# Making the remainder of each weight tile with an adding DMA instead of a subtraction

## The chip, the cores and the metric

The kernel runs on one core of a Trainium2 chip. The metric is the device time of one execution in microseconds; the time of a kernel is the median of several runs. Five engines work side by side, each through its own instructions in order: PE (matmul, with PEld for its weight loads), DVE (vector), ACT (scalar), POOL (GpSimd) and SP (which here only issues DMAs). POOL and ACT can issue DMAs too.

## The reference

The reference is the trunk of a two-layer transformer over 512 latent tokens and 256 context tokens, width 1024, in float32. Cut to its frame:

```
for layer in range(2):
    h_x = modulate(rmsnorm(x), ...);  h_c = modulate(rmsnorm(ctx), ...)
    o_x, o_c = attention(h_x @ w_in, h_c @ w_in) @ w_out
    x = x + gate * o_x
    h_x = modulate(rmsnorm(x), ...)
    x = x + gate * ((silu(h_x @ w1) * (h_x @ w3)) @ w2)
    if layer == 0:                      # the same two updates for ctx
        ...
return rmsnorm(x, final_g)
```

Layer 0 has two kinds of attention side by side (differential heads and neighbourhood heads), layer 1 a windowed grouped-query attention with sinks. The modulation vectors come from one matrix product per layer (`ada_w`).

## The kernel before

**Precision.** Each large matrix product in float32 is made of three matmuls in a rounded 32-bit format (`F32R` in the code, fp32r in the profile). A weight tile is split into a rounded part `wh` and a remainder `wl` = tile − `wh`; an activation is split likewise. `mm3` then adds up, for each block of 128 rows, `wh`·high (L157), `wh`·low (L158) and `wl`·high (L159). In the first attention unit the same three products stand as L475 to L477 (key, query) and L483 to L485 (value); for values L341 to L343.

**Weight tiles.** The class `Stream` brings all weights in one fixed order. A tile is 128 x 1024 floats, 512 KB. `request` issues its load on SP (L126) into a buffer `raw`; `make` splits it; `next` hands it out and keeps two tiles ahead of the matmuls (`ahead=2`). `wpool` has three buffers for each of `raw`, `wh` and `wl`; the tiles of `w2` have their own four buffers of `wh` and `wl`, but the same three of `raw`. A buffer of `wh` or `wl` comes free when PE has used the tile three places earlier; one of `raw` when the tile in it has been split. 184 tiles go this way: 24 of the input projection of layer 0 (`w_ab`), 8 and 8 of the two output projections, 12 of the input projection of layer 1, and 132 of the two feed-forward blocks (FFN): 22 hidden blocks j per layer, each with a tile of `w1`, of `w3` and of `w2`.

**The split before.** For each tile, ACT writes `wh` (L139, a rounding copy) and then the engine `eng` subtracts (L140). `eng` is DVE for 168 tiles, and GpSimd for 16: eight of `w_ab` (L413, L415), and `w1` and `w3` of j < 2 in each layer (L382).

**What else stands around it.** At the start, the modulation product for layer 0 (`ada_mm`, L172) uses raw tiles directly and shares the stream. Each norm goes through `rstd_of` (ACT L250, L252, L253; DVE L251, L254, L255) and `h_make`, which makes for each of eight row blocks the modulated input: DVE L295, ACT L296 (high part), DVE L297 (low part). POOL also has half of the rotation of queries and keys (L324, L325), bias tables for the neighbourhood heads (L690, L710, L711), scaling of softmax rows (L589, L733, L1173), and small DMAs. DVE adds results into the residual (L1009) and makes modulation rows of layer 1 beside other work (L206, L207).

**What sets the order.** The program is written as Python loops, and a scheduler with a timeline simulation then places all instructions of all engines (`schedule_with_timeline_sim=True`). Each engine runs its own list in order; an instruction that has to wait holds everything behind it on that engine.

Of the kernel before, what the change touches and what calls it, by code (L numbers as in the profile page):

```python
# [10 lines left out]
AF = mybir.ActivationFunctionType  # L11
ALU = mybir.AluOpType
# [20 lines left out]
def f32(ap):  # L33
    return ap.bitcast(F32)
# [3 lines left out]
def tile_trunk(  # L38
# [27 lines left out]
    nc = tc.nc  # L66
# [44 lines left out]
    class Stream:  # L111
# [17 lines left out]
        def make(self, upto):  # L129
            self.request(upto)  # L130
            while len(self.loaded) < min(upto, len(self.items)):
                raw, (_, kind, eng) = self.raws[len(self.loaded)], self.items[len(self.loaded)]
                if kind in ("ada", "raw"):
                    self.loaded.append(raw)
                    continue
                pool = wpool if kind == "w" else self.pools[kind]
                hi = pool.tile([P, 1024], F32R, tag=kind + "h", name="wh")
                lo = pool.tile([P, 1024], F32R, tag=kind + "l", name="wl")
                nc.scalar.copy(hi, raw)  # L139
                eng.tensor_sub(lo, raw, f32(hi))  # L140
                self.loaded.append((hi, lo))

        def next(self, ahead=2):
# [1276 lines left out]
```

## Time and profile before

| | us |
|---|---|
| median of three runs | 1698.72 (1695.31 to 1699.91) |
| profiled execution, its own time | 1692.1 |
| its span, first to last instruction | 1690.3 |
| PE busy | 1614.4 |
| DVE busy | 1082.7 |
| ACT busy | 622.9 |
| POOL busy | 271.8 |

The profile is of one execution, 6.6 us below the median. In its timeline rows stand the start in us from the start of the span, the duration in us, the engine, the line, the operation, the tile written and the tiles read, and in brackets how long the engine had been idle before and what ended that. The phases, by the lines that run: first projection and modulation to about 80 us, attention of layer 0 to about 350, its output projection to 484, FFN of layer 0 to about 1060, attention of layer 1 to about 1290, FFN of layer 1 to about 1640, final norm and output.

### The profile page before, as it was taken

What the parts mean: (1) busy time and instruction counts of PE and PEld (TensorE: products, weight loads), DVE (VectorE), ACT (ScalarE), POOL (GpSimd) and SP (SyncE); (2) the same over time, 40 slices, a digit from 0 to 9 for tenths busy, and PEclk for the clock granted to TensorE, in tenths of its full rate; (3) what the DMA queues carried; (4) which work ended last, traced back from release to release, by engine and by line L of the source; (5) the groups of instructions that cost most, each with busy time, mean ns of one, the idle gap of its engine ahead of it and who ended that gap; (6) DMA issues with size and microseconds to landing.
All of it is one profiled execution on the core that took longest, in us unless ns stands there. A gap on an engine that the chain in (4) does not pass through costs nothing.

```text
span 1690.3 us, 24508 instructions
## 1 busy us (share of the span) xinstructions
PE 1614.4 (96%) x9718; PEld 1383.0 (82%) x9718; DVE 1082.7 (64%) x1748; ACT 622.9 (37%) x1187; POOL 271.8 (16%) x287
## 2 busy tenths in 40 slices
PE   5899998999989999999999999999999999999997
PEld 3798978877878888888888887887788788888886
DVE  4758789956478676776776336778776654444444
ACT  4446545455243121121121133356665522222223
POOL 2223224643020000000000001255233000000001
PEclk9999999999999999999999999999999999999998
DMA  9312244543126333444433130311011533332221
GB/s 331 110 54 79 91 150 159 180 138 111 51 87 223 114 113 124 150 129 133 150 117 96 41 98 13 102 63 39 14 39 34 161 106 95 104 100 88 87 75 50
DMA packets 54746, 177.38 MB, mean 105 GB/s; under 512 B 6260, under 2 KB 10516, under 8 KB 54632
## 3 DMA queue, kind: packets, MB, share of 16 engines
q1 hardware_dynamic: 50760, 164.40, 30.7%
q0 software_dynamic: 3296, 10.89, 2.0%
q8 instruction: 76, 1.25, 0.3%
q10 hardware_dynamic: 576, 0.52, 0.1%
q14 instruction: 38, 0.31, 0.1%
HBM read 160.98 MB, written 4.86 MB: 98 GB/s over the span
## 4 chain that ended last, share of the span: by engine, by line
PE 66%; DVE 7%; DMA 3%; ACT 2%; issue 1%; POOL 0%; DVEq 0%; SPq 0%; ACTq 0%; POOLq 0%
PE f L157 16%; PE f L158 16%; PE f L159 16%; PE lin L157 3%; PE lin L159 3%; PE lin L158 3%; PE t L1196 2%; DMA raw<-in_w_dram 2%; PE t L1182 2%; DVE wl L140 1%; ACT wh L139 1%; DVE ns_h L295 1%; PE s L1158 1%; PE s L1156 1%; PE t L157 1%
## 5 line engine op out<-in xcount | busy, mean ns | idle before, releaser
L139 ACT CAST wh<-raw 128x1024 fp32r<-128x1024 f32 x184 | 192.1, 1049 | 688.8 <-PE f L158 489.9
L140 DVE TENSOR_TENSOR wl<-raw,wh 128x1024 fp32r<-128x1024 f32 x168 | 211.2, 1259 | 156.7 <-ACT wh L139 155.0
L157 PE MATMUL f<-hx,wh 128*128 128x512 f32 x704 | 273.9, 392 | 12.5 <-ACT hx L296 7.7
L158 PE MATMUL f<-hx,wh 128*128 128x512 f32 x704 | 272.7, 388 | 0.0
L159 PE MATMUL f<-hx,wl 128*128 128x512 f32 (+1 forms) x704 | 271.9, 387 | 0.0
L158 PE MATMUL f<-g,wh 128*128 128x512 f32 (+1 forms) x560 | 193.1, 345 | 0.0
L157 PE MATMUL f<-g,wh 128*128 128x512 f32 (+1 forms) x560 | 192.7, 346 | 0.0
L159 PE MATMUL f<-g,wl 128*128 128x512 f32 (+1 forms) x560 | 192.2, 343 | 0.0
L273 POOL TENSOR_TENSOR ns_a<-ns_a,ns_s 128x256 f32<-128x256 f32 (+1 forms) x20 | 19.3, 965 | 957.9 <-ACT ns_s L269 957.9
L1009 DVE SCALAR_TENSOR_TENSOR res<-f,mod,res 128x512 f32<-128x512 f32 (+1 forms) x248 | 152.7, 642 | 28.7 <-PE f L159 28.5
L157 PEld LDWEIGHTS f<-hx,wh 128*128 128x128 f32 x704 | 132.3, 189 | 41.8 <-ACT hx L296 8.1
L950 DVE TENSOR_TENSOR silu<-f,silu 128x768 f32<-128x768 f32 (+1 forms) x44 | 36.3, 824 | 202.1 <-PE f L159 196.4
L159 PEld LDWEIGHTS f<-hx,wl 128*128 128x128 f32 x704 | 132.4, 188 | 27.2
L158 PEld LDWEIGHTS f<-hx,wh 128*128 128x128 f32 x704 | 132.6, 188 | 25.3
L157 PEld LDWEIGHTS f<-g,wh 128*128 128x128 f32 x560 | 105.9, 190 | 14.1 <-issue 0.2
L158 PEld LDWEIGHTS f<-g,wh 128*128 128x128 f32 x560 | 106.1, 190 | 12.8 <-issue 0.2
L159 PEld LDWEIGHTS f<-g,wl 128*128 128x128 f32 x560 | 105.8, 189 | 13.0
L157 PE MATMUL lin<-hx,wh 128*128 128x512 f32 x272 | 110.0, 404 | 6.5 <-DVE q L314 2.6
L158 PE MATMUL f<-hc,wh 128*128 128x256 f32 x368 | 104.9, 286 | 3.4 <-DVE hc L297 3.4
L158 PE MATMUL lin<-hx,wh 128*128 128x512 f32 x272 | 107.4, 395 | 0.0
L159 PE MATMUL lin<-hx,wl 128*128 128x512 f32 x272 | 107.3, 394 | 0.0
L159 PE MATMUL f<-hc,wl 128*128 128x256 f32 x368 | 104.2, 285 | 0.0
(275 smaller groups left out, 3394.4 us busy)
## 6 DMA issues: line engine op xcount, KB each, us to landing
raw<-in_w_dram SPq DMA_DIRECT2D x132, 512.0 KB, 3.6
raw<-in_ada_wT_dram SPq DMA_DIRECT2D x80, 512.0 KB, 3.5
raw<-in_w_ab_dram SPq DMA_DIRECT2D x24, 512.0 KB, 4.0
raw<-in_ada_w_dram SPq DMA_DIRECT2D x16, 512.0 KB, 9.2
k<-k SPq DMA_DIRECT2D x16, 384.0 KB, 5.7
raw<-in_w_c_dram SPq DMA_DIRECT2D x12, 512.0 KB, 3.6
nb<-in_na_bias_dram POOLq DMA_DIRECT2D x16, 256.0 KB, 3.5
raw<-in_wo_ab_dram SPq DMA_DIRECT2D x8, 512.0 KB, 4.5
```

Source lines behind the costliest of these rows:

```text
L139: nc.scalar.copy(hi, raw)
L140: eng.tensor_sub(lo, raw, f32(hi))
L157: nc.tensor.matmul(ps, wh(k), xh(k), start=k == 0, stop=False)
L158: nc.tensor.matmul(ps, wh(k), xl(k), start=False, stop=False)
L159: nc.tensor.matmul(ps, wl(k), xh(k), start=False, stop=k == n - 1)
L273: nc.gpsimd.tensor_add(accs[e], accs[e], sq)
L295: nc.vector.scalar_tensor_tensor(ins[0], ins[1], amod[l][:, i, v, k : k + 1], ins[2], op0=ALU.mult, op1=ALU.mult)
L950: nc.vector.tensor_mul(s, ps[:, 0:nall], s)
L1009: evac[0] = nc.vector.scalar_tensor_tensor(res(m), ps[:, 0:n], mod[l][:, 5, v, m : m + 1], res(m), op0=ALU.mult, op1=ALU.add)
L1156: nc.tensor.matmul(s[:, 256:512], ql, k[:, kv, 0:NC], start=(n == 0), stop=(n == 1))
L1182: nc.tensor.transpose(t[:, k, :], d["p"][c][:, k * P : (k + 1) * P], ident)
L1196: nc.tensor.matmul(o[64 * c : 64 * c + 64, 0:P], v[:, kt, 64 * kv : 64 * kv + 64], pt[:, c, k, :], start=(k == 0), stop=(k == nb - 1),)
```

## The change

The remainder is no longer subtracted by an engine. ACT writes the negated rounded tile straight into `wl` (a pass of its own over the raw tile, scale −1, rounded to the same format), and a DMA issued by POOL then adds the raw tile onto it in SBUF: −round(raw) + raw. ACT still makes `wh` as before. The argument `eng` has no effect any more.

```
                 hi = pool.tile([P, 1024], F32R, tag=kind + "h", name="wh")
                 lo = pool.tile([P, 1024], F32R, tag=kind + "l", name="wl")
+                nc.scalar.activation(lo, raw, AF.Copy, scale=-1.0)
+                nc.gpsimd.dma_start(f32(lo), raw, accum_op=ALU.add)
                 nc.scalar.copy(hi, raw)
-                eng.tensor_sub(lo, raw, f32(hi))
                 self.loaded.append((hi, lo))
```

In the changed kernel the negating pass is L139, the DMA L140 and the copy to `wh` L141; every later line has a number one higher than before. The scheduler places all instructions anew. Three places follow; names carry the program's buffer numbers where rows would read alike, and "waits" lists what the instruction waits for (DMASW: a DMA issued by POOL, DMAHW: one issued by SP or ACT).

ACT in the norm ahead of the FFN of layer 0, before (`ns_t`, `ns_y`: the reciprocal root; `ns_s`: squares of the context's norm; `hx`: the modulated input):

```order
L250 ACTIVATE ns_t_4668<-t_4641,epst_98 128x512
L252 ACTIVATE ns_y_4667<-ns_t_4668 128x512
L139 CAST wh_4846<-raw_4838 128x1024
L253 ACTIVATE ns_t_4668<-ns_y_4667 128x512
L269 ACTIVATE ns_s_4896<-res_81 128x256
L269 ACTIVATE ns_s_4899<-res_82 128x256
L139 CAST wh_4850<-raw_4840 128x1024
L269 ACTIVATE ns_s_4902<-res_82 128x256
L296 ACTIVATE hx_4675<-ns_h_4683,mod0_117 128x512
```

and in the changed kernel:

```order
L251 ACTIVATE ns_t_4700<-t_4673,epst_98 128x512
L253 ACTIVATE ns_y_4699<-ns_t_4700 128x512
L141 CAST wh_4879<-raw_4870 128x1024
L139 ACTIVATE wl_4880<-raw_4870 128x1024
L254 ACTIVATE ns_t_4700<-ns_y_4699 128x512
L270 ACTIVATE ns_s_4931<-res_81 128x256
L270 ACTIVATE ns_s_4934<-res_82 128x256
L141 CAST wh_4884<-raw_4872 128x1024
L139 ACTIVATE wl_4885<-raw_4872 128x1024
L270 ACTIVATE ns_s_4937<-res_82 128x256
L297 ACTIVATE hx_4707<-ns_h_4715,mod0_117 128x512
```

The other rows keep their order; behind each copy to `wh` now stands the negating pass, one within the norm's chain and one ahead of the first `hx`.

POOL at the end of the first projection, before (`nb`: bias tables of the neighbourhood heads; `ru`, `rbuf`: rotation; `p`: softmax rows):

```order
L710 DMA nb<-in_na_bias_dram 128x2x256 [waits DMASW0_49]
L710 DMA nb<-in_na_bias_dram 128x2x256 [waits DMASW1_49]
L324 TENSOR_TENSOR ru<-ru,tables 128x512 [waits DVE_49]
L711 TENSOR_SCALAR nb<-nb 128x2x256 [waits DMASW0_49]
L325 TENSOR_TENSOR rbuf<-rbuf,ru 128x512 [waits DVE_49,Pool_49]
L711 TENSOR_SCALAR nb<-nb 128x2x256 [waits DMASW1_49]
L589 TENSOR_SCALAR p<-p,rs 128x768 [waits DVE_49]
```

and in the changed kernel:

```order
L711 DMA nb<-in_na_bias_dram 128x2x256 [waits DMASW3_49]
L711 DMA nb<-in_na_bias_dram 128x2x256 [waits DMASW4_49]
L325 TENSOR_TENSOR ru<-ru,tables 128x512 [waits DVE_49]
L712 TENSOR_SCALAR nb<-nb 128x2x256 [waits DMASW3_49]
L140 DMA wl<-raw 128x1024 [waits DMAHW2_49,DMASW0_49,Activation_49]
L326 TENSOR_TENSOR rbuf<-rbuf,ru 128x512 [waits DVE_49,Pool_49]
L712 TENSOR_SCALAR nb<-nb 128x2x256 [waits DMASW4_49]
L140 DMA wl<-raw 128x1024 [waits DMASW6_49,DMASW1_49,DMAHW3_49,PE_49,Activation_49]
L140 DMA wl<-raw 128x1024 [waits DMAHW4_49,DMASW2_49,Activation_49]
L140 DMA wl<-raw 128x1024 [waits DMASW5_49,DMAHW7_49,PE_49,Activation_49]
L590 TENSOR_SCALAR p<-p,rs 128x768 [waits DVE_49]
```

The first of these adding DMAs (that of the fourth weight tile) stands behind the first bias table, and each of the next three waits for its own negating pass ahead of the softmax row.

PE at the first projection tiles of layer 1, before (`t_9688`: keys of the latent tokens, `hx` the latent input, `hc` the context's; `wh_9674`, `wl_9675`: the key tile):

```order
L159 MATMUL t_9643<-hc_9456,wl_9367 128x256
L157 MATMUL t_9688<-hx_9185,wh_9674 128x512
L158 MATMUL t_9688<-hx_9185,wh_9674 128x512
L159 MATMUL t_9688<-hx_9185,wl_9675 128x512
L157 MATMUL t_9688<-hx_9186,wh_9674 128x512
```

and in the changed kernel (the key tile is `wh_9775`, `wl_9776`; `wh_9780` is the tile after it):

```order
L160 MATMUL t_9744<-hc_9557,wl_9465 128x256
L158 MATMUL t_9792<-hx_9283,wh_9775 128x512
L159 MATMUL t_9792<-hx_9283,wh_9775 128x512
L158 MATMUL lin_9865<-hx_9283,wh_9780 128x512
L159 MATMUL lin_9865<-hx_9283,wh_9780 128x512
L158 MATMUL t_9827<-hc_9550,wh_9775 128x256
L159 MATMUL t_9827<-hc_9550,wh_9775 128x256
L160 MATMUL t_9792<-hx_9283,wl_9776 128x512
```

Four matmuls that need no remainder moved ahead of the first that does.

More of the change, by code (lines that the diff above doesn't have):

```diff
@@ L138, in make @@
                 lo = pool.tile([P, 1024], F32R, tag=kind + "l", name="wl")
+                nc.scalar.activation(lo, raw, AF.Copy, scale=-1.0)
+                nc.gpsimd.dma_start(f32(lo), raw, accum_op=ALU.add)
                 nc.scalar.copy(hi, raw)
-                eng.tensor_sub(lo, raw, f32(hi))
                 self.loaded.append((hi, lo))
```

## The prediction

> **What bounds the kernel now.** I read the page first (busy times, then the chain that ended last), then the waits of PE, then the groups of the two lines of the split. The page:
>
> ```profile
> PE 1614.4 (96%) x9718; PEld 1383.0 (82%) x9718; DVE 1082.7 (64%) x1748; ACT 622.9 (37%) x1187; POOL 271.8 (16%) x287
> ...
> PE 66%; DVE 7%; DMA 3%; ACT 2%; issue 1%; POOL 0%; DVEq 0%; SPq 0%; ACTq 0%; POOLq 0%
> ...
> L139 ACT CAST wh<-raw 128x1024 fp32r<-128x1024 f32 x184 | 192.1, 1049 | 688.8 <-PE f L158 489.9
> L140 DVE TENSOR_TENSOR wl<-raw,wh 128x1024 fp32r<-128x1024 f32 x168 | 211.2, 1259 | 156.7 <-ACT wh L139 155.0
> ```
>
> PE is busy 1614.4 of 1690.3 us, so all its idle time is 76 us: no change that leaves the matmuls alone can gain more. The split's own engines have room, and the copy to `wh` mostly waits for PE (of 688.8 us idle ahead of it, 489.9 end when PE frees a buffer). The waits of PE:
>
> ```profile
> PE t L172 <- DMA raw<-in_ada_w_dram: 13.5, 2, 13.3
> PE f L157 <- ACT hx L296: 7.7, 2, 6.6
> ...
> PE f L157 <- DVE res L1009: 4.0, 7, 1.6
> ...
> PE s L485 <- DVE wl L140: 1.4, 1, 1.4
> ```
>
> 13.5 us are the first loads, which the change doesn't touch. Only 1.4 us wait for a remainder. So the removed work is nearly all hidden, and the question is which new latency is not.
>
> **What is removed and added.** 168 subtractions of 1259 ns leave DVE (211.2 us) and 16 leave POOL:
>
> ```profile
> L140 POOL TENSOR_TENSOR wl<-raw,wh x16: 2363/2393/3377, 183.5 to 1329.7; 128x1024 fp32r<-128x1024 f32 x16
> ```
>
> At the median of 2393 ns they are 38 us of POOL. ACT gets 184 passes; a negating pass isn't in the trace, the nearest row is the copy of the same shape, 1049 ns, so 193 us and ACT at about 816 us. For its room, two windows (length, then PE, PEld, DVE, ACT, POOL busy, clock, DMA share, GB/s):
>
> ```profile
> 200.00:350.00 150.00, 139.72 (x959) 123.22 (x957) 137.34 (x232) 77.50 (x177) 64.20 (x61) 0.99 0.51 162
> ...
> 1350.00:1640.00 290.00, 290.00 (x1281) 240.23 (x1280) 138.67 (x162) 75.46 (x90) 0.00 (x0) 1.00 0.31 97
> ```
>
> ACT is busy 75 of 290 us in the second FFN, where PE never idles, and 78 of 150 in the densest attention stage: there is room for a pass per tile.
>
> The adding DMA (POOL issues it, 512 KB from SBUF onto SBUF) is not in the trace. Its neighbours, KB each and us from issue to landing:
>
> ```profile
> raw<-in_w_dram SPq DMA_DIRECT2D x132, 512.0 KB, 3.6
> ...
> k<-k SPq DMA_DIRECT2D x16, 384.0 KB, 5.7
> ...
> csr<-crow_dram POOLq DMA_DIRECT2D x2, 512.0 KB, 6.8
> ...
> rbuf<-crow_dram POOLq DMA_DIRECT2D x1, 512.0 KB, 4.6
> ```
>
> Below it is bounded by the plain load, 3.6; above, if reading the destination came as a second transfer, by 3.6 + 6.8 = 10.4. I take a = 5.5 us from the end of the negating pass to landing, nearest to the copy within SBUF (5.7) and between the two loads that POOL issues. The Trainium skill, "DMA: Bandwidth & Descriptors", section on the anatomy of one DMA, puts a POOL-issued transfer at about 2.0 us + bytes/436 GB/s, an estimate of 3.2 us here; the four exposed places below would then lose 4 × 2.3 = 9.2 us less and the sum be near −1. The two 512 KB rows of POOL (4.6, 6.8) are above that.
>
> So `wl` is ready at copy 1.05 + pass 1.05 + 5.5 = 7.6 us after its buffers are free, against 1.05 + 1.26 = 2.3 before.
>
> **Where that is hidden.** The second FFN shows the rhythm:
>
> ```profile
> 1448.25 1.05 ACT L139 CAST wh<-raw 128x1024 fp32r<-128x1024 f32 x1 [3.62 <-PE f L158]
> ...
> 1456.41 1.05 ACT L139 CAST wh<-raw 128x1024 fp32r<-128x1024 f32 x1 [6.58 <-PE f L158]
> ```
>
> A buffer comes free every 8.16 us, and a tile is used two tiles later, 16.3 us: 7.6 fits, and even with a = 10.4 it takes 12.5. The three raw buffers serve six loads (two each of `w1`, `w3`, `w2`) in four such periods, 32.6 us; one cycle is load 3.6 + 2.1 + 5.5 = 11.2, so 6 × 11.2/3 = 22.4 us. Raw buffers bind only from a cycle of 16.3, that is a = 10.6. The first FFN has half as much matmul again per tile (context columns). Here I cost the change at nothing; PE's matmuls are the cover.
>
> **Where it is exposed.** At four places PE comes to the remainder just after it is made.
>
> (1) Start, 25 to 48 us. First matmul and the wait that follows it:
>
> ```profile
> 26.98 0.49 PE L475 MATMUL lin<-hx,wh 128*128 128x512 f32 x1 [2.47 <-ACT hx L296]
> ...
> 29.29 0.79 PE L476 MATMUL lin<-hx,wh 128*128 128x512 f32 x1 [1.81 <-DVE hx L297]
> ```
>
> ACT's negating pass stands ahead of `hx`, about +1; the remainders come some 4 us later, but the new order gives PE five of the eight second modulation groups meanwhile. I take +1.5 (0 to +4).
>
> (2) The fourth tile, 63 to 73 us:
>
> ```profile
> 62.93 1.05 ACT L139 CAST wh<-raw 128x1024 fp32r<-128x1024 f32 x1
> ...
> 65.95 1.11 POOL L711 TENSOR_SCALAR nb<-nb 128x512 f32<-128x512 f32 x1 [0.65 <-DVE k L314]
> ...
> 66.38 0.28 PE L483 MATMUL s<-wh,hx 128*128 128x256 f32 x1
> 66.50 0.28 PE L484 MATMUL s<-wh,hx 128*128 128x256 f32 x1
> ...
> 68.19 0.39 PE L485 MATMUL s<-wl,hx 128*128 128x256 f32 x1 [1.41 <-DVE wl L140]
> ```
>
> The pass ends at about 65.0, but POOL's list has the DMA behind the bias row that ends at 67.06: landing 72.6. PE starved from 66.6 before (the second L484 starts 0.12 us after its neighbour); the new order puts 14 matmuls of this width and two of twice the width ahead, 2.2 us, to about 68.8. Idle 3.8 instead of 1.4: +2.5.
>
> (3) First key tile of layer 1, about 1080 us:
>
> ```profile
> 1079.03 1.05 ACT L139 CAST wh<-raw 128x1024 fp32r<-128x1024 f32 x1 [2.75 <-PE t L342]
> ...
> 1081.39 0.50 PE L159 MATMUL t<-hx,wl 128*128 128x512 f32 x1
> ```
>
> Pass 1080.1 to 1081.1, landing 1086.6, against 1081.4; the four matmuls moved ahead cover 0.7: +4.5.
>
> (4) `w1`, `w3` of j = 1 in the second FFN, about 1330 us:
>
> ```profile
> 1328.61 1.05 ACT L139 CAST wh<-raw 128x1024 fp32r<-128x1024 f32 x1 [3.12 <-PE f L158]
> ...
> 1329.73 2.38 POOL L140 TENSOR_TENSOR wl<-raw,wh 128x1024 fp32r<-128x1024 f32 x1 [17.99 <-ACT wh L139]
> ...
> 1332.66 0.40 PE L159 MATMUL f<-hx,wl 128*128 128x512 f32 x1
> ```
>
> One activation stands between copy and pass, which ends at 1331.1; landing 1336.6 against a use at 1332.66: +3.9.
>
> Sum of the four 12.4; each us of a moves it by 4. To this I add +2 (0 to +10) for POOL waiting in order: each adding DMA waits for its pass, with rotation and softmax rows behind it (the 200 to 350 row has POOL busy 64 of 150 us, so most such waits have room). The Trainium skill, "SBUF — State Buffer", section on who interferes with whom, says that a DVE copy or tensor_scalar in its two-port mode starves POOL of the ports with which it makes DMA descriptors, which speaks against moving work to POOL-issued DMAs. An estimate by it: one more DVE row of 0.7 us on each of four places, +2.8; no row of the trace of before shows it either way.
>
> **What is gained.** POOL's subtractions run with DVE rows stretched beside them. The longest stall that isn't a load is such a place:
>
> ```profile
> 475.46 0.63 ACT L253 ACTIVATE ns_t<-ns_y 128x512 f32<-128x512 f32 x1
> ...
> 475.63 2.39 POOL L140 TENSOR_TENSOR wl<-raw,wh 128x1024 fp32r<-128x1024 f32 x1 [1.33 <-ACT wh L139]
> ...
> 476.47 2.11 DVE L254 SCALAR_TENSOR_TENSOR ns_t<-ns_t,ns_v 128x512 f32<-128x512 f32 x1
> ...
> 479.12 2.51 POOL L140 TENSOR_TENSOR wl<-raw,wh 128x1024 fp32r<-128x1024 f32 x1
> ...
> 479.36 2.82 DVE L255 SCALAR_TENSOR_TENSOR ns_y<-ns_t,ns_y 128x512 f32<-128x512 f32 x1
> ...
> 484.05 0.80 PE L157 MATMUL f<-hx,wh 128*128 128x512 f32 x1 [6.58 <-ACT hx L296]
> ...
> 22.27 0.69 DVE L254 SCALAR_TENSOR_TENSOR ns_t<-ns_t,ns_v 128x512 f32<-128x512 f32 x1 [0.63 <-ACT ns_t L253]
> ```
>
> The last row is the same operation without POOL beside it. Two such rows lose 1.4 + 2.1 = 3.5; ACT's new pass within the chain costs 1.05 back. I take −2.5 (0 to −5). In the attention of layer 0, DVE is busy 137 of 150 us and PE idles 10; DVE loses some 15 subtractions there and six of POOL's neighbours: −3 (0 to −6). The residual adds that PE waits for (4.0 us) come earlier without subtractions ahead of them: −1 (0 to −2). At the start of the second FFN, DVE rows are stretched likewise but the remainder comes later by about as much: 0. Gains −6.5 together.
>
> **Sum.** +12.4 + 2 − 6.5 = +7.9. The profiled execution of 1692.1 us would become 1700.0; it lies 6.6 below the median, so against the median the forecast is 1698.7 + 7.9 = 1706.6.
>
> **Rivals.**
> - *DVE and POOL are freed, and the DMA is quick: faster.* With a = 3.6 the four places cost 12.4 − 7.6 = 4.8, nothing is lost to POOL's order, and the gains are at their ends, −13: −8.2, or 1690.5. With such gains the change pays below a = 5.65 (12.4 + 4 × 0.15 = 13); with the gains that I took only below 3.5. For it: the stretched rows on the longest chain, the load row of 3.6. Against: the 5.7 of the copy within SBUF.
> - *The adding DMA is slow.* With a = 10.4 the four places lose 4 × 4.9 = 19.6 more, +27.5: 1726; past 10.6 the raw buffers bind as well, 2 us per group for each us. For it: destination read and written, 96 MB more through the DMA engines. Against: their share was 0.31 in the FFN.
> - *POOL's queue holds the softmax.* If half of the 28 tiles split during the two attentions (20 of `w_ab` after the first four, 8 of layer 1) hold POOL's chain for one ACT pass, 14 × 1.05 = 14.7 in place of my 2, +20.6: 1719.
> - *Nothing shows.* PE's cover takes it all: 1699. This is also what a scheduler order that hides all four places would give.
>
> **How the numbers follow.** The forecast has 0.50 (own range +1 to +14, 1700 to 1713), the quick DMA 0.25, the slow one 0.13, the held queue 0.07, nothing 0.05. A difference of 0.3% (5.1 us) is about what can be told from none: bounds 1693.6 and 1703.8. Of the forecast 0.30 lies above, 0.20 within; of the quick DMA 0.22 below, 0.03 within. So slower 0.30 + 0.13 + 0.07 = 0.50, same 0.20 + 0.03 + 0.05 = 0.28, faster 0.22. The range from 1690 (the quick DMA's own time) to 1726 (the slow one's) leaves out about 2 in 10.
>
> **What would show it.** The DMA group of L140 gives a directly: 5.5 is right, 4 or below the first rival, 9 or above the second. PE's waits should name the DMA for `wl` at about 40, 70, 1085 and 1335 us, some 4 us each, and hardly any in the FFNs. The wait on `hx` at 484 should shrink from 6.6 to about 3.6, and the rows L255, L256 there be 0.7. POOL rows L590 or L1174 ended by ACT's L139 show the held queue. Wrong I am above all if the four places are hidden by another order, or if the DMA is so slow that PE waits for it in the FFN.

## The result and the profile after

The changed kernel takes 1769.08 us (median of four runs, 1765.02 to 1770.22) against 1698.9 us for the kernel before (four runs by then): a ratio of 1.0414, 95% interval 1.0389 to 1.0439. It is 70 us slower, well outside the forecast of 1706.6 and its range of 1690 to 1726. The profiled execution took 1765.0 us, 72.9 more than that of before.

The page of the changed kernel (busy times; the chain that ended last; the split's lines; the DMA queues with packets, MB and share of the 16 engines; issues with KB each and us to landing):

```profile
PE 1643.6 (93%) x9718; PEld 1397.7 (79%) x9718; DVE 869.4 (49%) x1580; ACT 791.7 (45%) x1371; POOL 377.6 (21%) x455
...
q0 software_dynamic: 29792, 107.38, 32.1%
q1 hardware_dynamic: 50760, 164.40, 28.2%
...
PE 55%; DMA 11%; DVE 5%; issue 3%; ACT 2%; POOL 0%; SPq 0%; DVEq 0%; ACTq 0%; POOLq 0%
...
L141 ACT CAST wh<-raw 128x1024 fp32r<-128x1024 f32 x184 | 191.1, 1043 | 392.8 <-PE f L159 296.0
...
L139 ACT ACTIVATE wl<-raw 128x1024 fp32r<-128x1024 f32 x184 | 194.2, 1056 | 224.6 <-DMA raw<-in_w_dram 223.7
...
wl<-raw POOLq DMA_DIRECT2D x184, 512.0 KB, 5.5
raw<-in_w_dram SPq DMA_DIRECT2D x132, 512.0 KB, 4.7
```

The two new prices are close to what the prediction took: the pass 1056 ns, the adding DMA 5.5 us from issue to landing (4.5 to 10.7). Yet PE is idle 119.6 us (span 1763.2 less 1643.6) where it was idle 75.9. What ACT waits for has shifted. Before, its work on a weight tile waited 489.9 us for PE to free a buffer and 134.6 us for the *load* of a raw tile of the FFN:

```profile
ACT wh L139 <- DMA raw<-in_w_dram: 134.6, 40, 6.1
```

Now it is 296.0 us for PE and 256.1 for that load (223.7 ahead of the pass, 32.4 ahead of the copy). The loads themselves have become slower, 4.7 us in the median where they took 3.6. And hardly any of PE's own waits name the remainder, 9.5 us in eight waits (the largest groups of PE's waits: us in total, times, longest):

```profile
PE t L173 <- DMA raw<-in_ada_w_dram: 17.2, 7, 13.2
PE f L158 <- DVE res L1010: 13.7, 5, 7.4
PE s L613 <- DMA k<-k: 7.5, 2, 6.3
...
PE t L160 <- DMA wl<-raw: 4.3, 2, 3.0
PE f L160 <- DMA wl<-raw: 4.2, 5, 1.9
PE lin L158 <- DVE q L315: 4.1, 1, 4.1
PE f L158 <- ACT hx L297: 3.5, 1, 3.5
```

Where PE falls behind can be read by counting: both kernels run 9718 matmuls, so the start of the n-th in one trace is set against the n-th in the other. The table gives by how many us the lag grows in each stretch (times are those of the kernel before); the other columns are experiments told below. The trace of before is of an execution 6.6 us below the median, so the sums come out some us above the differences of the medians; and a control that changes only the second FFN (e16, below) grows or shrinks by up to 2.2 us in stretches ahead of it, so a difference of 2 us is not to be read.

| stretch of before, us | changed | e3 pass | e7 `wh` | e8 hold | e10 hold, add | e11 both | e5 HBM | e12 spared | e15 buffers |
|---|---|---|---|---|---|---|---|---|---|
| 13–47 start | 10.3 | 0.0 | −0.5 | 0.0 | −0.4 | 0.8 | 12.1 | −0.1 | 11.2 |
| 47–200 | 0.3 | 2.7 | 2.8 | 0.3 | 4.5 | 2.9 | 6.4 | 1.9 | 1.0 |
| 200–385 attention, layer 0 | 28.8 | 11.0 | 8.6 | 12.2 | 20.2 | 25.1 | 16.4 | 22.9 | 24.7 |
| 385–544 with the norm | −2.8 | 2.4 | 1.3 | 0.5 | −0.2 | 0.5 | 3.0 | −2.8 | −2.7 |
| 544–578 start of FFN 0 | 14.6 | 0.0 | 0.0 | 7.5 | 13.3 | 22.3 | 0.1 | 8.5 | 16.1 |
| 578–1022 rest of FFN 0 | −2.9 | −5.5 | −2.8 | −2.9 | 56.5 | 82.6 | 14.2 | −1.6 | −0.4 |
| 1022–1090 first tiles, layer 1 | 5.8 | −0.4 | −1.1 | −0.4 | 0.3 | 0.6 | 6.8 | −1.0 | 6.6 |
| 1090–1323 | 0.8 | 3.7 | 5.9 | 3.6 | 11.9 | 9.2 | 4.1 | 1.5 | 13.6 |
| 1323–1340 `w1`, `w3` of j = 1 | 5.5 | 1.5 | 0.0 | 0.0 | 0.0 | 4.1 | 8.1 | 0.4 | 5.7 |
| 1340–1377 next tiles | 11.2 | 0.0 | 0.0 | 5.2 | 17.3 | 15.9 | 2.9 | 3.9 | 0.0 |
| 1377–1680 rest of FFN 1 | 1.7 | 0.0 | 0.9 | 0.0 | 5.2 | 10.2 | 5.1 | 7.3 | 0.2 |
| lag at the last matmul | 73.2 | 15.0 | 15.7 | 25.4 | 127.7 | 173.4 | 78.5 | 40.3 | 75.6 |

How a late load becomes an idle PE is seen at the start of the first FFN, in the chain of work that ends with PE's longest wait for a residual add (start, us, what):

```profile
552.03 10.10 DMA wl<-raw
562.13 0.02 SPq L126
...
562.18 4.91 DMA raw<-in_w_dram
...
568.08 1.03 ACT wh L141
569.11 0.75 ACT g L153
...
574.68 9.27 DMA raw<-in_ada_wT_dram
...
587.00 4.70 DMA raw<-in_w_dram
...
591.72 1.07 ACT wl L139
...
593.07 6.97 DMA wl<-raw
600.04 0.02 SPq L126
...
600.09 5.17 DMA raw<-in_w_dram
...
606.29 1.05 ACT wl L139
607.34 0.74 ACT g L153
...
608.11 0.96 DVE g L154
609.06 0.67 DVE res L1010
...
609.78 0.80 PE f L158
```

Read from the top: an adding DMA lands, and only then SP may issue the next load into that raw buffer; ACT waits in order for that load, and the activation of an FFN block (`g`, L153), which has nothing to do with it, stands behind. SP's list is in order too, so a modulation row's load that has to wait for its own buffer holds the next weight load; here an earlier row (`in_ada_wT`) took 9.27 us to land (4.5 in the median), and DVE had to use it before a buffer came free. Then the circle load, ACT, adding DMA, load, ACT runs once more; DVE gets its input, frees the accumulator, and PE goes on after 7.42 us.

### The profile page after: what moved, and what is told of

It is laid out like the page before. It is cut to its first block, busy times and chain, and to the rows that moved or that the text cites. A ratio compares the mean times of both kernels' runs of the same rounds, so it can differ in the third digit from the quotient of the medians.

```text
span 1763.2 us, 24886 instructions
## 1 busy us (share of the span) xinstructions
PE 1643.6 (93%) x9718; PEld 1397.7 (79%) x9718; DVE 869.4 (49%) x1580; ACT 791.7 (45%) x1371; POOL 377.6 (21%) x455
## 3 DMA queue, kind: packets, MB, share of 16 engines
q0 software_dynamic: 29792, 107.38, 32.1%
## 4 chain that ended last, share of the span: by engine, by line
PE 55%; DMA 11%; DVE 5%; issue 3%; ACT 2%; POOL 0%; SPq 0%; DVEq 0%; ACTq 0%; POOLq 0%
PE f L158 13%; PE f L159 13%; PE f L160 13%; DMA wl<-raw 5%; DMA raw<-in_w_dram 3%; PE t L1197 2%; PE lin L158 2%; PE lin L159 2%; PE lin L160 2%; DMA raw<-in_ada_wT_dram 2%; PE t L1183 2%; DVE junk L207 1%; ACT wl L139 1%; PE s L1159 1%; PE s L1157 1%
## 5 line engine op out<-in xcount | busy, mean ns | idle before, releaser
L141 ACT CAST wh<-raw 128x1024 fp32r<-128x1024 f32 x184 | 191.1, 1043 | 392.8 <-PE f L159 296.0
L140 POOL DMA_DIRECT2D wl<-raw x184 | 161.4, 877 | 945.1 <-ACT wl L139 867.4
L139 ACT ACTIVATE wl<-raw 128x1024 fp32r<-128x1024 f32 x184 | 194.2, 1056 | 224.6 <-DMA raw<-in_w_dram 223.7
L158 PE MATMUL f<-g,wh 128*128 128x512 f32 (+1 forms) x560 | 196.0, 351 | 15.9 <-DVE res L1010 11.9
L159 PE MATMUL f<-g,wh 128*128 128x512 f32 (+1 forms) x560 | 195.4, 349 | 0.0
L158 PE MATMUL lin<-hx,wh 128*128 128x512 f32 x272 | 112.4, 413 | 9.0 <-DVE q L315 4.1
L159 PEld LDWEIGHTS f<-g,wh 128*128 128x128 f32 x560 | 107.7, 192 | 13.3 <-issue 0.2
L159 PE MATMUL lin<-hx,wh 128*128 128x512 f32 x272 | 109.0, 401 | 0.0
```

The source lines that it names most:

```text
L139: nc.scalar.activation(lo, raw, AF.Copy, scale=-1.0)
L140: nc.gpsimd.dma_start(f32(lo), raw, accum_op=ALU.add)
L158: nc.tensor.matmul(ps, wh(k), xh(k), start=k == 0, stop=False)
L159: nc.tensor.matmul(ps, wh(k), xl(k), start=False, stop=False)
```

## The experiments

All are timed against the kernel before on the same chip; ratios have 95% intervals.

**One part of the tiles at a time.** e1 uses the new split for the 52 projection tiles only, e2 for the 132 FFN tiles only (`new` stands for the one test that differs).

```
+                if new(tile):        # e1: projections, e2: FFN
+                    nc.scalar.activation(lo, raw, AF.Copy, scale=-1.0)
+                    nc.gpsimd.dma_start(f32(lo), raw, accum_op=ALU.add)
+                    nc.scalar.copy(hi, raw)
+                else:
+                    nc.scalar.copy(hi, raw)
+                    eng.tensor_sub(lo, raw, f32(hi))
```

> The adding DMA for the 52 projection tiles only; the 132 FFN tiles are split by subtraction as before. In the trace of the changed kernel PE falls behind at four stretches: +10 us before 47 us, +29 between 205 and 390, +13 at 557 to 567 (first FFN), +16 at 1330 to 1370 (second FFN). Theory H (hold): the raw buffer, one of three, is held until the adding DMA lands, so the next load on SP's queue and what stands behind it come late; it expects the first two stretches and the step at 1080 to stay and the FFN ones to go: 1698.9 + 10 + 30 + 5 = 1744 (1732 to 1752). Theory L (late remainder: PE waits for wl itself): all waits for wl in the trace are 9.5 us, so at most 1708. Theory T (total load: passes on ACT, traffic of the DMAs): 52 of 184 tiles, 0.28 of 70 us, 1719.

> The adding DMA for the 132 FFN tiles only; the 52 projection tiles are split by subtraction as before. H: only the two FFN starts stay: 1699 + 13 + 16 = 1728 (1715 to 1735). L: about half of the 9.5 us of waits for wl are in the second FFN: 1704. T: 132 of 184 tiles, 0.72 of 70 us: 1749.

Measured: e1 1741.02 us (1.0268, 1.0237 to 1.0298), e2 1715.27 us (1.0103, 1.0084 to 1.0122). e1 meets the hold theory and lies far from the figures of the other two. e2 lies at the lower edge of the hold theory's range, above the late remainder alone and far from the total load. The lags of the two traces are 44.7 and 21.7 us, together 66.4 of 73.2, and each sits in its own stretches: the loss is local, not a tax on every tile.

**The pass on ACT alone, and a plain copy that holds the raw buffer.** e3 adds the negating pass to the kernel before, e4 a plain DMA of each raw tile to scratch in HBM.

```
# e3
+                nc.scalar.activation(lo, raw, AF.Copy, scale=-1.0)
                 nc.scalar.copy(hi, raw)
                 eng.tensor_sub(lo, raw, f32(hi))
# e4
                 nc.scalar.copy(hi, raw)
                 eng.tensor_sub(lo, raw, f32(hi))
+                dump = dpool.tile([P, 1024], F32, tag="dump", name="dump", bufs=6)
+                nc.gpsimd.dma_start(dump, raw)
```

> The kernel before with ACT's negating pass added ahead of the rounding copy, its result overwritten by the old subtraction; no adding DMA. It doubles ACT's work per tile and lengthens the split by 1.05 us. H and L: within +10 us (raw held 1 us longer instead of 5): 1700 to 1709. If ACT's extra 193 us were the cause, most of the 70 us: 1740 or more.

> The kernel before with a plain DMA added that reads each raw tile and writes it to a scratch buffer in HBM, issued by POOL; the remainder is made by subtraction as before, so it is not late. The raw buffer is held until that DMA lands, some 4 to 5 us after it may start, against 2.3 us. H: a part of the 70 us, at the same stretches, 1715 to 1745. L: no change, 1699. T: the traffic is the same in bytes, so about the DMA part of the 70 us, spread over all stretches with many tiles.

Measured: e3 1708.5 us (1.0065, 1.0044 to 1.0086), e4 1709.06 us (1.0066, 1.0048 to 1.0083). The pass costs 11 us, at the upper edge of what was expected and mostly in the attention of layer 0, where the prediction had costed it at nothing. e4 fell short of the hold theory's 1715: its DMA lands 3.3 us after issue and may start before the subtraction (it only reads the raw tile), so it hardly holds the buffer longer.

**Without the hold.** e5 is the changed kernel with the adding DMA reading HBM.

```
-                nc.gpsimd.dma_start(f32(lo), raw, accum_op=ALU.add)
+                nc.gpsimd.dma_start(lo, src.bitcast(F32R), accum_op=ALU.add)
```

> The changed kernel, but the adding DMA reads the weight tile from HBM again instead of from the raw buffer. The raw buffer is free after ACT's two passes; ACT's work, the order on POOL and the late remainder stay, and HBM traffic grows by 96 MB. H (the raw buffer is held until the add lands, loads and what is queued behind them come late): most of the 70 us come back, 1705 to 1720, the rest being the passes on ACT (+11 in the run with the pass alone) and the four places with a late remainder. L (late remainder): no change, 1769. T (traffic): no change or worse, 1769 to 1790.

Measured: 1768.52 us (1.0429, 1.0404 to 1.0454), a clear miss for the hold theory as I had put it. The trace says why the time doesn't move (issues, us to landing):

```profile
raw<-in_w_dram SPq DMA_DIRECT2D x132, 512.0 KB, 6.4
wl<-in_w_dram POOLq DMA_DIRECT2D x132, 512.0 KB, 7.4
```

The remainder takes 7.4 us instead of 5.5, the loads 6.4 instead of 4.7. In the table, the start of FFN 0 comes back whole (14.6 to 0.1), 12 us of the attention and 8 of the second FFN's start do too; as much is lost in other stretches (start, rest of FFN 0, second FFN), where the slower transfers are the likely reason. So the hold is one cause of several, and this run doesn't size it.

**The GpSimd subtractions alone.** e6 is the kernel before with `nc.vector.tensor_sub` for all 184 tiles.

> The kernel before, with the 16 subtractions that ran on GpSimd moved to DVE; no adding DMA, no further pass. It measures by itself the gain that the prediction took from DVE rows no longer stretched beside POOL's subtractions: by the prediction's terms 5.5 us (2.5 + 1.05 in the norm, 3 in the attention of layer 0, less some 2 for DVE's 16 subtractions more): 1692 to 1696. If DVE's load in the attention is the limit instead, 1699 to 1705.

Measured: 1688.33 us (0.9951, 0.9931 to 0.9972), 8 us faster than the kernel before, a little more than expected. The norm ahead of the first FFN shows 2.2 us of it: DVE's two rows there take 0.83 and 0.68 us (2.11 and 2.82 before), the wait on `hx` 4.4 us instead of 6.6. Where the rest comes from was not followed up.

```profile
479.14 0.83 DVE L254 SCALAR_TENSOR_TENSOR ns_t<-ns_t,ns_v 128x512 f32<-128x512 f32 x1
480.29 0.68 DVE L255 SCALAR_TENSOR_TENSOR ns_y<-ns_t,ns_y 128x512 f32<-128x512 f32 x1
```

**The hold without the rest.** e7 copies `wh` to HBM instead of the raw tile (same bytes, no hold). e8 copies the raw tile, but only after the remainder is made: a POOL copy of one column from `wl` into the dead raw tile orders it. e10 is e8 with an adding DMA onto the scratch (the first six tiles are written plainly); e11 is e10 with the negating pass as well.

```
                 nc.scalar.copy(hi, raw)
                 eng.tensor_sub(lo, raw, f32(hi))
+                nc.gpsimd.dma_start(dump, f32(hi))                       # e7
+                nc.gpsimd.tensor_copy(raw[:, 0:1], f32(lo)[:, 0:1])      # e8, e10, e11
+                nc.gpsimd.dma_start(dump, raw)                           # e8
+                nc.gpsimd.dma_start(dumps[n % 6], raw, accum_op=ALU.add) # e10, e11
```

> The kernel before plus a plain DMA per tile that reads the rounded part wh (not the raw tile) and writes it to scratch in HBM, issued by POOL. The same bytes as in the run with the plain copy of the raw tile (+12 us), but the raw buffer is not held by it; wh is needed by PE much longer anyway. H (hold): 1697 to 1702, so the +12 was the hold. T (traffic): about +12, 1709.

> The kernel before plus, per tile: a one-column POOL copy from wl into the dead raw tile, then a plain DMA from the raw tile to scratch in HBM. So the DMA starts only after the remainder is made and the raw buffer is held for the whole of it, about as long as by the adding DMA, while the remainder itself is on time and ACT has no further pass. H: 1735 to 1760, at the same stretches as the changed kernel. L: 1699 to 1705. T: as in the plain copy, about 1709.

> As the full hold, but the DMA adds the raw tile onto its scratch in HBM instead of writing it (all but the first six), so its packets should take about 340 ns like those of the adding DMA in the changed kernel, not 159. The remainder is on time and there is no further pass. H, with the longer transfer: 1725 to 1745, the full hold's 1717 and more, at the attention of layer 0 and the FFN starts, nothing at the start. If the length of the transfer doesn't matter: 1717.

> The run before plus the negating pass on ACT ahead of the rounding copy (overwritten by the subtraction): all that the change adds except that the remainder comes from the DMA. H plus pass: the sum of both, 1740 to 1760. What is left to the changed kernel's 1769 is the late remainder and the order that the scheduler builds on it: L in its weak form expects at least 15 us left, H none.

Measured: e7 1704.7 us (1.0048, 1.0032 to 1.0063), e8 1716.71 us (1.0111, 1.0092 to 1.013), e10 1818.33 us (1.0724, 1.0692 to 1.0756), e11 1874.13 us (1.1042, 1.1008 to 1.1076). All four lie outside what I wrote. e7's 8 us are neither theory's figure, but its column is a control for the others: its loads land as late as those of the changed kernel (4.6 us), no load waits for its DMA, and it loses 0.0 us at both FFN starts and 8.6 in the attention. So slower transfers alone cost nothing at the FFN starts, where e8 loses 7.5 and 5.2 by the hold; in the attention most of e8's 12.2 may not be the hold. e8 and e10 differ in an adding DMA in place of a writing one, and that turns +20 into +121 us: the buffer is held 5.5 us from issue instead of 3.2, and the DMA engines are taken twice as long (33.0% of them against 16.3%); the runs don't part these two. DVE's waits in e10 point to why it overshoots the changed kernel:

```profile
DVE wl L140 <- ACT wh L139: 323.7, 83, 11.4
```

Here the remainder still comes from DVE, so DVE too stands in order behind a late load (155.0 us before), with the residual adds behind it. In the changed kernel DVE has no such wait. e10 and e11 show that a raw buffer released late, with the remainder on time, is enough to lose time at both FFN starts and loses none at the program's start; they are not the changed kernel's size.

**Sparing the places.** e12 is the changed kernel with 17 of 184 tiles split by subtraction on DVE; e9 uses the new split only for the FFN blocks j > 5 and DVE for the rest.

> The changed kernel with 17 of 184 tiles split by subtraction on DVE: the first five, the first four of layer 1's projection, and w1, w3 of hidden blocks 0 and 1 in both FFNs. These are the places where PE comes to a remainder soon after it is made. If late remainders and the order built on them matter there: back by 10 (start) + 5 (1080) + 15 to 25 (FFN starts) = 1729 to 1739. H alone, with the hold spread over all tiles: back by 17/184 of 70 to 15, 1754 to 1762.

> The adding DMA only for the FFN tiles of hidden blocks j > 5 in both layers (96 of 184), all other tiles by subtraction on DVE. The prediction cost the steady part of an FFN at nothing, and the trace of the changed kernel shows PE falling back by nothing there. H and L: as the run with all subtractions on DVE, 1688 (1684 to 1696). T: 96 of 184 tiles of 70 us, 1725.

Measured: e12 1731.43 us (1.0218, 1.0185 to 1.0251): 17 tiles bring back about half of the 70 us (34 are left), in the table the start (10.3 to −0.1), the step at 1080 (5.8 to −1.0), that at 1330 (5.5 to 0.4) and part of the bursts at both FFN starts (14.6 to 8.5, 11.2 to 3.9); of the attention's 28.8 us 22.9 stay. e9 1687.1 us (0.9945, 0.9923 to 0.9966): 96 tiles with the adding DMA in the steady part of the FFNs cost nothing against e6. Both e6 and e9 beat both kernels, the kernel before by half a per cent; they can't be told apart.

**More raw buffers.** e13 gives `w2` a raw buffer of its own in both FFNs, taking one from the modulation rows; e14 is the same in the kernel before. e15 and e16 give `w2` three further ones in the second FFN, where there is room.

```
+                if kind == "w2" and self.pools.get("raw2"):   # e15, e16
+                    raw = self.pools["raw2"].tile([P, 1024], F32, tag="raw2", name="raw")
...
+        S.pools["raw2"] = st.enter_context(tc.tile_pool(name="f_raw2", bufs=3))
```

> The changed kernel with a raw buffer of its own for the w2 tiles in both FFNs, so that the three shared ones serve only w1 and w3 there; to make room, the modulation rows that run beside the first FFN have one buffer instead of two. The adding DMA and the late remainder are as in the changed kernel. H: the 14.6 us at the start of the first FFN and most of the 15.7 at the second come back: 1741 to 1757. L: 1769.

> The same two edits in the kernel before, as the control: H and L both expect 1692 to 1704, since there the raw buffers come free 2.3 us after they are loaded and PE waited for no weights.

> The changed kernel with three raw buffers of their own for the w2 tiles in the second FFN alone; nothing is taken away for them. H (shortage of raw buffers): of the 15.7 us that PE falls behind from 1313 to 1399 us of the kernel before, 8 to 13 come back, 1756 to 1761. L (late remainder): 1767 to 1771, the 15.7 us stay.

> The same buffers in the kernel before, as the control: 1695 to 1700, since its second FFN has no idle PE to win.

Measured: e13 1797.9 us (1.0601, 1.0574 to 1.0629) and e14 1721.4 us (1.0154, 1.0126 to 1.0181). The control itself loses 27 us (15.5 of them at the start of FFN 0, where the modulation rows have the single buffer), so the pair tells nothing about the hold in the first FFN. In the second, where only `w2`'s own buffer is new, e13 falls back 0.0 us between 1340 and 1377 (the changed kernel 11.2, e14 0.0). e15 1766.16 us (1.0415, 1.0391 to 1.0439), e16 1699.44 us (1.0018, 1.0008 to 1.0028): by its total e15 goes to the late remainder (0.8 us below its range), but the table takes it apart. With enough buffers the 11.2 us at 1340 to 1377 are 0.0, as in e13, so that part was the shortage; the 5.5 us at 1330 stay, 5.7. What was won is lost again earlier, where the free buffers let eight loads go out within 26 us while the last projection tile's remainder was still to be made; its adding DMA took 8.5 us to land (window of e15):

```profile
1339.09 26.03 SPq L129 DMA_DIRECT2D raw<-in_w_dram  x8
...
1357.29 0.58 PE L163 MATMUL t<-hx,wl 128*128 128x256 f32 x1 [6.27 <-DMA wl<-raw]
```

## Why the prediction was wrong, by its own steps

- **Prices: right, but for one.** The pass was to be 1049 ns and is 1056; ACT's sum was to be about 816 us and is 791.7; a was to be 5.5 us and is 5.5 from issue, 5.8 from the end of the pass (4.8 to 11.0). So the quick and the slow DMA are both out; the estimate of 3.2 us fits the writing DMA of e8 (3.2), not the adding one. What the sum left at its old price is the weight load: 4.7 us beside the adding DMAs, 3.6 before.
- **"Here I cost the change at nothing; PE's matmuls are the cover": the step that failed.** It held for the steady part of the FFNs (−2.9 and +1.7 us; e9), for which it was worked out. It was carried to every tile outside the four places. The loads of an FFN's first blocks come in a burst, and in the attention of layer 0 the same three raw buffers also carry modulation rows, so an average cycle (22.4 of 32.6 us) says nothing there. 28.8 us were lost in the attention, 14.6 and 11.2 at the FFN starts: 54.6 of 73.2. At the starts it is the held raw buffer: the loss is 0.0 with the pass alone (e3) and with slower loads alone (e7), it comes with a hold and a punctual remainder (e8, e10), and it goes when the hold goes (e5: 14.6 to 0.1, 11.2 to 2.9) or the buffers suffice (e15, e13: 11.2 to 0.0).
- **"There is room for a pass per tile": failed in the attention.** The mean of 78 of 150 us hid a place without room. The net 28.8 us contain one step of 10.7, between 248 and 260 us of the kernel before. Every run with the pass on these tiles has it (e3 8.6, e5 9.6, e11 9.9, e15 10.3, e12 12.1); without the pass no run loses more than 3.3 there (e6; e4 0.6, e7 0.7, e8 −0.7, e10 0.6). So the step belongs to the pass, with the order built around it. In the changed kernel copy and pass stand ahead of an activation (`sn_q`) for which PE waits:

```profile
266.55 1.05 ACT L141 CAST wh<-raw 128x1024 fp32r<-128x1024 f32 x1
267.50 1.06 ACT L139 ACTIVATE wl<-raw 128x1024 fp32r<-128x1024 f32 x1
268.46 0.83 ACT L664 ACTIVATE sn_q<-at 128x768 f32<-128x768 f32 x1
...
269.34 2.93 PE L247 MATMUL t<-sn_q,ones 128*128 128x384 f32 x4 [2.86 <-ACT sn_q L664]
```

  How the other 18 us of the attention divide between the hold, the slower transfers (8.6 in e7) and the new order is not settled.
- **What carries it: in-order lists.** I named POOL's list as the one to watch (+2, 0 to +10). The ones that the traces show at work are SP's, where a load that waits for a buffer holds the next loads and copies, and ACT's, where a pass that waits for a load holds activations and norms. PE's longest wait of the attention is such a case, for a copy of `k` (6.35 us, shown below): SP's list was held until 226.2 and 228.7 us, when two adding DMAs landed, and the copies went out behind the loads:

```profile
226.27 0.33 SPq L126 DMA_DIRECT2D raw<-in_w_ab_dram  x1
228.75 0.80 SPq L126 DMA_DIRECT2D raw<-in_ada_wT_dram  x2
229.61 0.47 SPq L330 DMA_DIRECT2D k<-k  x1
230.13 0.59 SPq L331 DMA_DIRECT2D k<-k  x1
```

  Beside these loads the second copy took 9.2 us to land (median before 5.7). On POOL's list, the other engines' waits for the softmax rows of L590 and L1174 are 13.4 us in all, 10.1 before; the held-queue rival had put 14.7 us there.
- **Place 1, the start: mis-sized.** Predicted +1.5 (0 to +4), measured +10.3. I counted the modulation groups that PE has meanwhile as cover, but their loads wait for raw buffers that the adding DMAs hold. SP waits 13.3 us for them in the first 60 us:

```profile
SPq L126 <- DMA wl<-raw: 13.3, 3, 6.3
```

  In the following rows of PE (start and length of eight-matmul groups) each group waits for its load, while the first remainder had already landed (issued at 25.9 us, landed at 34; the first three adding DMAs take 8.0 to 10.0 us each). PE comes to it, in the last row, only at 45.8:

```profile
39.04 1.08 PE L173 MATMUL t<-raw,csil 128*32 128x256 f32 x8 [0.31 <-DMA raw<-in_ada_w_dram]
...
41.98 0.64 PE L173 MATMUL t<-raw,csil 128*32 128x256 f32 x8 [1.86 <-DMA raw<-in_ada_w_dram]
43.45 1.08 PE L173 MATMUL t<-raw,csil 128*32 128x256 f32 x8 [0.83 <-DMA raw<-in_ada_w_dram]
...
45.81 0.80 PE L478 MATMUL lin<-hx,wl 128*128 128x512 f32 x1
```

  With the same hold but a punctual remainder and the old order (e8, e10) nothing is lost here, and with the hold gone but the new order (e5) it is all lost. That points to the order that the scheduler built on a late remainder (in e12, with the first five tiles subtracted, the start is back at −0.1); the order by itself wasn't tried.
- **Places 3 and 4: right.** +4.5 and +3.9 predicted, +5.8 and +5.5 measured; both stay when the hold is gone (e5: 6.8 and 8.1) and vanish in e12. Place 2 (+2.5) doesn't show (+0.3 in its stretch).
- **Gains: the norm right, the rest not seen.** −2.5 predicted for the norm, −2.8 measured, with the wait on `hx` down from 6.6 to 3.5 us. The −3 in the attention can't be seen beside the loss there, and the −1 at residual adds didn't come: PE waits 13.7 us for those adds, against 4.0.
- **The range** took the slow rival's raw buffers to bind only from a = 10.6, the same average cycle again; so it ended at 1726.

Not in the prediction at all: idle PE time costs more than itself. Of the 72.9 us that the span grew, 43.7 are idle and 29.2 are PE being busy longer with the same matmuls at a lower mean granted clock (0.969 against 0.989). After the wait at 239.5 us, matmuls of 512 columns start 0.43 us apart until 244.6, then 0.23:

```profile
239.51 0.55 PE L613 MATMUL s<-k,q 128*128 128x256 f32 x1 [6.35 <-DMA k<-k]
...
241.14 0.63 PE L159 MATMUL lin<-hx,wh 128*128 128x512 f32 x1
241.57 0.63 PE L160 MATMUL lin<-hx,wl 128*128 128x512 f32 x1
...
245.39 0.40 PE L158 MATMUL lin<-hx,wh 128*128 128x512 f32 x1
245.62 0.39 PE L159 MATMUL lin<-hx,wh 128*128 128x512 f32 x1
```

The Trainium skill, "TensorE: Matmul & The Clock Gate", section on the oscillation of the clock gate, has the rule that PE should have no idle gap of more than about 3.4 us, since the clock then falls to half; these rows agree (6.35 us idle, then 0.43 us from start to start in place of 0.23). By this one place, an estimate: a stall of 6 us costs some 2.4 us on top ((244.6 − 239.5) × (0.43 − 0.23)/0.43).

## What to carry to other kernels

Price a slower producer by how long it keeps its *input* buffer, too, not only by when its output is ready; then follow that buffer to the next load and to everything queued in order behind whoever waits for it. An average cycle that fits in the steady part says nothing of bursts or of stages where the ring serves other transfers, and a mean busy share says nothing of the one place where an added pass stands ahead of what PE waits for. Where a subtraction on a second engine disturbs the first, moving the few instructions back can win what a new mechanism was to bring: here e6 won 8 us.

## What the hardware showed that I had not expected

In these runs an adding DMA occupied the DMA engines twice as long as a writing one. For the same packets and the same 107.38 MB, POOL's queue has a share of 32.1% of the engines in the changed kernel and 33.0% of e10's longer span, against 16.3% in e8:

```profile
q0 software_dynamic: 29792, 107.38, 16.3%
```

Issued in the same way from the same buffer, 512 KB land after 3.2 us written (e8) and 5.5 us added (e10). Reading the raw tile from HBM for the addition made it 7.4 us and slowed the ordinary loads beside it from 4.7 to 6.4 us (e5).
